# First-layer modulation columns: summed over the condition by TensorE, tile by tile, in place of VectorE, ScalarE and GpSimd

## The chip, the cores and the metric

The kernel runs on one core of one Trainium2 chip. The metric is device time in microseconds of one execution, lower is better. Engines are named as in the profile: PE is TensorE's products and PEld its weight loads, DVE is VectorE, ACT is ScalarE, POOL is GpSimd, SP is SyncE, which issues all the transfers.

## The reference

An encoder of two layers over 2048 tokens of 1024 channels. What matters here is the first step of a layer: a condition vector gives a shift and a scale for each channel and a gate.

```python
cond = jax.nn.silu(c)
for l in range(DEPTH):
    mod = cond @ ada_w[l] + ada_b[l]
    shift, scale, gate = jnp.split(mod, 3, axis=-1)
    h = x * (1.0 + scale[:, None]) + shift[:, None]
    ...
    x = layer_norm(DEEPNORM_ALPHA * x + (1.0 + gate[:, None]) * y, ln_g[l], ln_b[l])
```

`ada_w[l]` is 1024 x 3072. The first 2048 columns of `mod` are shift and scale; nothing of layer 0 can be multiplied before they are known. The projection of `h` that follows goes into two mixers (a gated linear recurrence and an RWKV-like one), and layer 1 is a gated recurrence behind a short convolution.

## The kernel before

Tokens go in two super-blocks of 1024, each in two halves (b = 0, 1) of 512; channels in eight tiles of 128 (k = 0 to 7). Each large product is done as three fast-float products of split operands (`mm3`, L431 to L433: high and low parts of both sides), so each input tile `h` is split into `hh` and `hl` by ScalarE and VectorE (`split`, L367 and L368) before TensorE may use it.

The start, which the change touches, is written in this order. A small matrix `wf` is folded from the low-rank weights: 32 f32 products of 256 columns into `pf` (L239), evacuated by ScalarE (L243). Then the columns of `ada_w[0]` come in four blocks of 512 columns (j), eight tiles `adw` of 128 x 512 f32 (256 KB) per block: blocks 0 and 2 first (shift and scale of channel tiles 0 to 3), then six x tiles, then blocks 1 and 3 (channel tiles 4 to 7), then the other x tiles. All are issued by SyncE in that order; 20 buffers hold `adw`, so the 21st tile waits until the first is used up.

`mod_start(j)` (L202) sums a block over the condition. Rows of a tile lie on partitions and one value of `cond` belongs to each, so a multiply by a per-partition scalar and an add over k leave a 128 x 512 sum per block: five of the eight k go through VectorE's multiply-add (`mod_add`, L166 and L168), three through ScalarE (L211, L213), two of which GpSimd adds up (L214), and VectorE joins both (L215). `mod_vec` (L186) then sums over the partitions on TensorE: four f32 products whose weights are 128 x 128 pieces of the sum and whose moving operand is one column of ones (L190). The result `pm`, 128 x 4, gets the bias in `mod_bias` (L175) and lies in `md`, from which ScalarE makes `h` (L401).

TensorE records two loads and two products for one such f32 product, so a call of `mod_vec` shows as eight records of each kind. The order on TensorE within a mixer is written by hand; at the start it is the scheduler's, from the order of the code and its priorities. The first projections are `pp_z` (96 products: two halves of the weights, two column tiles, two token halves); the first 18 need only blocks 0 and 2. The gate columns of layer 0 (blocks 4 and 5) and all of layer 1 keep the old way, later (`mod_cols`, L178, beside the mixer).

Of the kernel before, what the change touches and what calls it, by code (L numbers as in the profile page):

```python
# [13 lines left out]
F32 = mybir.dt.float32  # L14
# [3 lines left out]
AF = mybir.ActivationFunctionType  # L18
# [5 lines left out]
P = 128  # L24
D = 1024
KT = 8
BLK = 512
# [41 lines left out]
def tile_encoder(  # L69
# [19 lines left out]
    nc = tc.nc  # L89
# [27 lines left out]
    tp = _Cur()  # L117
    ps = ctx.enter_context(tc.tile_pool(name="ps", bufs=1, space=PSUM))
# [39 lines left out]
    cond = cst.tile([P, KT], F32, name="cond")  # L158
# [5 lines left out]
    def mod_add(acc, w, k, first):  # L164
        if first:
            nc.vector.tensor_scalar_mul(acc, w, cond[:, k : k + 1])  # L166
        else:
            nc.vector.scalar_tensor_tensor(  # L168
                out=acc, in0=w, scalar=cond[:, k : k + 1], in1=acc, op0=ALU.mult, op1=ALU.add
            )  # L170

    def mod_bias(l, j, pm):
        js = slice(4 * j, 4 * j + 4)
        o = VOFF[f"adb{l}"] + 4 * j
        nc.vector.scalar_tensor_tensor(  # L175
            out=md[l][:, js], in0=pm, scalar=0.0 if j < 2 else 1.0, in1=vec[:, o : o + 4], op0=ALU.add, op1=ALU.add
        )
# [8 lines left out]
    def mod_vec(l, j, acc):  # L186

        pm = ps.tile([P, 4], F32, name=f"pm{l}_{j}", tag="ta")
        for i in range(4):
            nc.tensor.matmul(pm[:, i : i + 1], acc[:, i * P : (i + 1) * P], ones, start=True, stop=True)  # L190
        mod_bias(l, j, pm)
# [9 lines left out]

    def mod_start(j):  # L202

        acc = [tp.tile([P, BLK], F32, name=f"acc0_{j}_{i}", tag=f"acc{i}", bufs=2) for i in range(2)]
        for k in range(KT):
            w = tp.tile([P, BLK], F32, name=f"adw0_{j}_{k}", tag="adw", bufs=20)
            nc.sync.dma_start(w, ada_w[0, k * P : (k + 1) * P, j * BLK : (j + 1) * BLK])
            if k not in (0, 2, 4):
                mod_add(acc[0], w, k, first=k == 1)
            elif k == 0:  # L210
                nc.scalar.activation(acc[1], w, AF.Identity, scale=cond[:, 0:1])  # L211
            else:
                nc.scalar.activation(w, w, AF.Identity, scale=cond[:, k : k + 1])  # L213
                nc.gpsimd.tensor_add(acc[1], acc[1], w)  # L214
        nc.vector.tensor_add(acc[0], acc[0], acc[1])  # L215
        return acc[0]

    x_first = []

    def x_tile(sb, b, k):  # L220
        src = up.tile([P, BLK + 3], F32, name=f"xt{sb}_{b}_{k}", tag="u")[:, 0:BLK]
        t0 = sb * SBT + b * BLK
        nc.sync.dma_start(src, xT[k, :, t0 : t0 + BLK])
        return src
# [11 lines left out]
    for k in range(KT):  # L236
# [5 lines left out]
            )  # L242
        nc.scalar.copy(wf[:, :, k], pf)  # L243

    accs = {j: mod_start(j) for j in (0, 2)}
    for j in (0, 2):
        mod_vec(0, j, accs[j])
    x_first += [x_tile(0, 0, k) for k in range(4)]
    x_first += [x_tile(0, 1, k) for k in range(2)]

    accs = {j: mod_start(j) for j in (1, 3)}
    for j in (1, 3):
        mod_vec(0, j, accs[j])

    def late_modulation_steps(l, js):

# [1109 lines left out]
```

## Time and profile before

| | us |
|---|---|
| median of three runs | 2450.46 |
| lowest and highest | 2445.37, 2455.84 |
| the profiled execution | 2446.24 |
| its span, first to last instruction | 2444.5 |
| TensorE busy in it | 2208.4 |
| mean granted TensorE clock (1 is 2.4 GHz) | 0.952 |

The profile is of one execution. Times in it are counted from the start of the span. A busy TensorE includes overlapped records, and a granted clock of 0.50 in a stretch means 1.2 GHz; a value between is a stretch in which it changed.

### The profile page before, as it was taken

To read this page: it belongs to the slowest core of one execution; us is meant where nothing else is said; L and a number is where in the kernel's file an instruction comes from. 1 tells how busy PE (TensorE), PEld (TensorE's weight loads), DVE (VectorE), ACT (ScalarE), POOL (GpSimd) and SP (SyncE) were. 2 spreads that over 40 slices of the span, in tenths; PEclk is the share of its full clock that TensorE was granted. 3 is DMA by queue.
4 is the path that set the end of the run, shared out by engine and by line. 5 is a ranking of instruction groups with operands and counts; after the bars stand their busy time and mean duration, and the time that the engine had idled before them with its cause. 6 is when DMAs were issued, how large, how long until landed. Compare 5 with 4: busy or idle time off the path is not lost. (4 is left out here: it accounts for less than half of the span.)

```text
span 2444.5 us, 45532 instructions
## 1 busy us (share of the span) xinstructions
PE 2208.4 (90%) x18400; PEld 1738.7 (71%) x18400; DVE 1454.8 (60%) x2697; ACT 1256.6 (51%) x2027; POOL 557.2 (23%) x586
## 2 busy tenths in 40 slices
PE   5989989999987998899999999989986999996998
PEld 4767767677766876677776777768765778774776
DVE  6546667566644677565666755356766156766166
ACT  4344556545566433454455556654666344666332
POOL 3311112111112222111111111122433232433231
PEclk7989999999998999999999999989998999998999
DMA  7310111111424645111111123254313544113542
GB/s 289 93 37 24 41 32 41 38 38 38 118 70 128 207 152 175 34 34 43 25 42 35 37 83 97 72 204 143 104 65 120 169 141 137 67 57 122 167 137 103
DMA packets 185938, 229.82 MB, mean 94 GB/s; under 512 B 65912, under 2 KB 99320, under 8 KB 185728
## 3 DMA queue, kind: packets, MB, share of 16 engines
q1 hardware_dynamic: 185728, 226.92, 29.1%
q8 instruction: 144, 2.36, 0.4%
q14 instruction: 66, 0.54, 0.1%
HBM read 175.46 MB, written 51.39 MB: 93 GB/s over the span
## 5 line engine op out<-in xcount | busy, mean ns | idle before, releaser
L431 PE MATMUL pp_g<-hl_h,wh_g 128*128 128x512 f32 x512 | 212.3, 415 | 40.8 <-ACT go L574 40.8
L433 PE MATMUL pp_g<-hh_h,wl_g 128*128 128x512 f32 x512 | 204.6, 400 | 2.0 <-POOL wl_g L368 2.0
L431 PE MATMUL po<-hl_wo,wh_mx 128*128 128x512 f32 x448 | 179.3, 400 | 28.9 <-DVE hl_wo L368 24.1
L432 PE MATMUL pp_g<-hh_h,wh_g 128*128 128x512 f32 x512 | 204.9, 400 | 0.0
L433 PE MATMUL po<-hh_wo,wl_mx 128*128 128x512 f32 x448 | 177.4, 396 | 0.0
L432 PE MATMUL po<-hh_wo,wh_mx 128*128 128x512 f32 x448 | 177.2, 396 | 0.0
L368 POOL TENSOR_TENSOR wl_g<-raw_g,wh_g 128x512 fp32r<-128x512 f32 x64 | 87.2, 1363 | 377.5 <-ACT wh_g L367 342.7
L431 PE MATMUL pp_b<-hl_h,wh_b 128*128 128x512 f32 x384 | 168.5, 439 | 5.0 <-ACT cr_b L805 5.0
L431 PE MATMUL pp_a<-hl_h,wh_a 128*128 128x512 f32 x384 | 168.7, 439 | 0.0
L432 PE MATMUL pp_b<-hh_h,wh_b 128*128 128x512 f32 x384 | 153.7, 400 | 0.0
L433 PE MATMUL pp_a<-hh_h,wl_a 128*128 128x512 f32 x384 | 153.5, 400 | 0.0
L432 PE MATMUL pp_a<-hh_h,wh_a 128*128 128x512 f32 x384 | 153.3, 399 | 0.0
L433 PE MATMUL pp_b<-hh_h,wl_b 128*128 128x512 f32 x384 | 153.0, 398 | 0.0
L431 PEld LDWEIGHTS pp_g<-hl_h,wh_g 128*128 128x128 f32 x512 | 99.5, 194 | 64.7 <-ACT go L574 41.7
L368 POOL TENSOR_TENSOR wl_a<-raw_a,wh_a 128x512 fp32r<-128x512 f32 x48 | 67.7, 1416 | 329.1 <-ACT wh_a L367 329.1
L568 DVE TENSOR_TENSOR go<-go,oi 128x512 f32<-128x512 f32 x64 | 46.8, 733 | 160.6 <-ACT go L564 144.9
L368 POOL TENSOR_TENSOR wl_mx<-raw_mx,wh_mx 128x512 fp32r<-128x512 f32 x64 | 80.7, 1265 | 269.1 <-ACT wh_mx L367 269.1
L368 POOL TENSOR_TENSOR wl_b<-raw_b,wh_b 128x512 fp32r<-128x512 f32 x48 | 66.5, 1391 | 271.1 <-ACT wh_b L367 270.1
L431 PEld LDWEIGHTS po<-hl_wo,wh_mx 128*128 128x128 f32 x448 | 86.0, 192 | 48.4 <-DVE hl_wo L368 24.9
L433 PEld LDWEIGHTS pp_g<-hh_h,wl_g 128*128 128x128 f32 x512 | 99.2, 194 | 25.2 <-POOL wl_g L368 3.5
L432 PEld LDWEIGHTS pp_g<-hh_h,wh_g 128*128 128x128 f32 x512 | 99.4, 194 | 19.2
L433 PE MATMUL pp_c<-hh_h,wl_c 128*128 128x512 f32 x256 | 102.2, 400 | 8.6 <-POOL wl_c L368 8.6
(355 smaller groups left out, 5707.4 us busy)
## 6 DMA issues: line engine op xcount, KB each, us to landing
adw<-in_ada_w_dram SPq DMA_DIRECT2D x96, 256.0 KB
oi<-o_dr SPq DMA_DIRECT2D x64, 256.0 KB
m_dr<-go SPq DMA_DIRECT2D x56, 256.0 KB
raw_b<-in_w_ev_dram SPq DMA_DIRECT2D x48, 256.0 KB
raw_a<-in_w_ev_dram SPq DMA_DIRECT2D x48, 256.0 KB
raw_g<-in_w_ev_dram SPq DMA_DIRECT2D x32, 256.0 KB
wo<-in_w_evo_dram SPq DMA_DIRECT2D x32, 256.0 KB
raw_mx<-m_dr SPq DMA_DIRECT2D x32, 256.0 KB
```

Of the source, the lines that this page charges most:

```text
L368: return (eng or nc.vector).tensor_tensor(out=lo, in0=src, in1=hi.bitcast(F32), op=ALU.subtract)
L431: nc.tensor.matmul(pt, ah, bl, start=first, stop=False)
L432: nc.tensor.matmul(pt, ah, bh, start=False, stop=False)
L433: nc.tensor.matmul(pt, al, bh, start=False, stop=last)
L568: nc.vector.tensor_mul(go[b], go[b], oi[b])
```

## The change

`mod_start` no longer makes a 128 x 512 sum. Each tile is used as weights as it lies: its four 128 x 128 pieces are loaded, the moving operand is column k of `cond`, and the eight k add up in the PSUM tile `pms`, 128 x 4. The bias goes on as before. Each block has a PSUM tag of its own, and `mod_vec` is no longer called for blocks 0 to 3 of layer 0.

```diff
     def mod_start(j):
 
-        acc = [tp.tile([P, BLK], F32, name=f"acc0_{j}_{i}", tag=f"acc{i}", bufs=2) for i in range(2)]
+        pm = ps.tile([P, 4], F32, name=f"pms_{j}", tag=("ta", "oa", "yb", "cg")[j])
         for k in range(KT):
             w = tp.tile([P, BLK], F32, name=f"adw0_{j}_{k}", tag="adw", bufs=20)
             nc.sync.dma_start(w, ada_w[0, k * P : (k + 1) * P, j * BLK : (j + 1) * BLK])
-            if k not in (0, 2, 4):
-                mod_add(acc[0], w, k, first=k == 1)
-            elif k == 0:
-                nc.scalar.activation(acc[1], w, AF.Identity, scale=cond[:, 0:1])
-            else:
-                nc.scalar.activation(w, w, AF.Identity, scale=cond[:, k : k + 1])
-                nc.gpsimd.tensor_add(acc[1], acc[1], w)
-        nc.vector.tensor_add(acc[0], acc[0], acc[1])
-        return acc[0]
+            for i in range(4):
+                nc.tensor.matmul(
+                    pm[:, i : i + 1], w[:, i * P : (i + 1) * P], cond[:, k : k + 1],
+                    start=k == 0 and i == 0, stop=k == KT - 1, skip_group_check=True,
+                )
+        mod_bias(0, j, pm)
...
-    accs = {j: mod_start(j) for j in (0, 2)}
     for j in (0, 2):
-        mod_vec(0, j, accs[j])
+        mod_start(j)
...
-    accs = {j: mod_start(j) for j in (1, 3)}
     for j in (1, 3):
-        mod_vec(0, j, accs[j])
+        mod_start(j)
```

The order that results, on TensorE, from the last fold to the first projection. Names carry layer or block and k (`adw0_0_1` is tile 1 of block 0), then a buffer number. Before:

```order
L239 MATMUL pf7_171<-lw_114,zw2_112 128x256
L239 MATMUL pf7_171<-lw_114,zw3_113 128x256
L190 MATMUL pm0_0_235<-ones_91,acc0_0_0_177 128x1 [waits DVE_49]
L190 MATMUL pm0_0_235<-ones_91,acc0_0_0_177 128x1 x3
L190 MATMUL pm0_2_241<-ones_91,acc0_2_0_206 128x1 [waits DVE_49,PE_49]
L190 MATMUL pm0_2_241<-ones_91,acc0_2_0_206 128x1 x3
L431 MATMUL pp_z0_1_0_547<-hl_h0_0_0_0_388,wh_z0_1_0_356 128x512 [waits DVE_49]
```

Changed, the last of the 16 tiles of blocks 0 and 2 and what follows:

```order
L209 MATMUL pms_2_227<-cond_106,adw0_2_6_264 128x1 [waits DMAHW4_49]
L209 MATMUL pms_2_227<-cond_106,adw0_2_6_264 128x1 x3
L209 MATMUL pms_2_227<-cond_106,adw0_2_7_270 128x1 [waits DMAHW5_49]
L209 MATMUL pms_2_227<-cond_106,adw0_2_7_270 128x1 x3
L426 MATMUL pp_z0_1_0_607<-hl_h0_0_0_0_448,wh_z0_1_0_416 128x512 [waits DVE_49]
L427 MATMUL pp_z0_1_0_607<-hh_h0_0_0_0_432,wh_z0_1_0_416 128x512 [waits Activation_49]
L428 MATMUL pp_z0_1_0_607<-hh_h0_0_0_0_432,wl_z0_1_0_417 128x512 [waits Pool_49]
L209 MATMUL pms_1_289<-cond_106,adw0_1_0_290 128x1 [waits DMAHW4_49]
L209 MATMUL pms_1_289<-cond_106,adw0_1_0_290 128x1 x3
L426 MATMUL pp_z0_1_0_607<-hl_h0_0_0_1_449,wh_z0_1_0_416 128x512
```

Where two bursts of four products stood, waiting for VectorE, there are now 64 products, each tile's first one waiting for its transfer; two of them stand earlier, between the second and the third fold. Six tiles of blocks 1 and 3 lie between the first 18 projections, the other ten stand behind them.

On VectorE, the last block before the split of the second token half (b = 1, k = 3). Before:

```order
L168 SCALAR_TENSOR_TENSOR acc0_3_0_288<-adw0_3_7_313,cond_106,acc0_3_0_288 128x512 [waits DMAHW3_49,DVE_49]
L215 TENSOR_TENSOR acc0_3_0_288<-acc0_3_0_288,acc0_3_1_289 128x512 [waits DVE_49,Pool_49]
L175 SCALAR_TENSOR_TENSOR md0_108<-pm0_3_323,vec_104 128x4 [waits PE_49]
L367 CAST hh_h0_0_1_3_383<-xt0_1_3_427 128x512 [waits Activation_49]
```

Changed:

```order
L363 TENSOR_TENSOR hl_h0_0_1_0_456<-xt0_1_0_285,hh_h0_0_1_0_440 128x512 [waits Activation_49]
L175 SCALAR_TENSOR_TENSOR md0_108<-pms_1_289,vec_104 128x4 [waits PE_49]
L175 SCALAR_TENSOR_TENSOR md0_108<-pms_3_339,vec_104 128x4 [waits PE_49]
L362 CAST hh_h0_0_1_3_443<-xt0_1_3_487 128x512 [waits Activation_49]
```

The adds are gone; the two writes of `md` follow one another directly, ahead of the split of tile 3 as the last one was before.

## Rows read from the trace of the kernel before

**Rows 1.** The page: span and instructions, then busy us of each engine.
```profile
span 2444.5 us, 45532 instructions
...
PE 2208.4 (90%) x18400; PEld 1738.7 (71%) x18400; DVE 1454.8 (60%) x2697; ACT 1256.6 (51%) x2027; POOL 557.2 (23%) x586
```

**Rows 2.** Timeline of PE: start us, length us, instructions, [idle before, who ended it].
```profile
9.34 15.06 PE L239 MATMUL pf<-lw,zw 128*128 128x256 f32 x60 [1.28 <-DMA zw<-in_w_zT_dram]
24.25 0.95 PE L190 MATMUL pm<-ones,acc 128*128 128x1 f32 x8
29.57 1.80 PE L190 MATMUL pm<-ones,acc 128*128 128x1 f32 x8 [4.37 <-DVE acc L215]
34.96 0.79 PE L431 MATMUL pp_z<-hl_h,wh_z 128*128 128x512 f32 x1 [3.60 <-DVE hl_h L368]
35.55 0.63 PE L432 MATMUL pp_z<-hh_h,wh_z 128*128 128x512 f32 x1
35.98 0.63 PE L433 MATMUL pp_z<-hh_h,wl_z 128*128 128x512 f32 x1
...
42.70 0.40 PE L433 MATMUL pp_z<-hh_h,wl_z 128*128 128x512 f32 x1
42.93 0.40 PE L431 MATMUL pp_z<-hl_h,wh_z 128*128 128x512 f32 x1
...
47.18 1.84 PE L190 MATMUL pm<-ones,acc 128*128 128x1 f32 x8 [3.06 <-DVE acc L215]
53.20 1.84 PE L190 MATMUL pm<-ones,acc 128*128 128x1 f32 x8 [4.18 <-DVE acc L215]
```

**Rows 3.** The same of PEld, TensorE's weight loads in three of the four bursts.
```profile
24.03 1.08 PEld L190 LDWEIGHTS pm<-ones,acc 128*128 128x128 f32 x8
29.54 1.74 PEld L190 LDWEIGHTS pm<-ones,acc 128*128 128x128 f32 x8 [4.43 <-issue]
...
47.15 1.78 PEld L190 LDWEIGHTS pm<-ones,acc 128*128 128x128 f32 x8 [3.75 <-issue]
```

**Rows 4.** The same of VectorE, to 94 us.
```profile
27.86 1.56 DVE L215 TENSOR_TENSOR acc<-acc,acc 128x512 f32<-128x512 f32 x1
31.40 0.16 DVE L175 SCALAR_TENSOR_TENSOR md<-pm,vec 128x4 f32<-128x4 f32 x1 [1.98 <-PE pm L190]
...
55.07 0.16 DVE L175 SCALAR_TENSOR_TENSOR md<-pm,vec 128x4 f32<-128x4 f32 x1 [2.02 <-PE pm L190]
...
92.38 0.75 DVE L797 SCALAR_TENSOR_TENSOR u_b<-pp_b,vec,u_b 128x511 f32<-128x511 f32 x1
93.04 1.53 DVE L168 SCALAR_TENSOR_TENSOR acc<-adw,cond,acc 128x512 f32<-128x512 f32 x2
```

**Rows 5.** Groups by line, 0 to 57 us: count, busy us, mean ns, idle before.
```profile
L168 DVE SCALAR_TENSOR_TENSOR acc<-adw,cond,acc 128x512 f32<-128x512 f32 x16 | 17.9, 1121 | 1.8 <-DMA adw<-in_ada_w_dram 1.5
...
L214 POOL TENSOR_TENSOR acc<-acc,adw 128x512 f32<-128x512 f32 x8 | 12.0, 1500 | 22.9 <-ACT adw L213 22.8
```

**Rows 6.** SyncE's queue: start us, us, transfers issued.
```profile
21.89 10.39 SPq L207 DMA_DIRECT2D adw<-in_ada_w_dram  x16
```

**Rows 7.** Stretches: length, busy us (records) by engine, granted clock, DMA share, GB/s.
```profile
29.50:30.00 0.50, 0.43 (x3) 0.46 (x3) 0.00 (x0) 0.00 (x0) 0.50 (x1) 0.62 1.07 393
...
39.00:40.00 1.00, 1.00 (x4) 0.63 (x2) 1.00 (x1) 1.00 (x3) 0.92 (x2) 0.57 1.06 389
40.00:41.00 1.00, 0.24 (x2) 0.00 (x0) 1.00 (x2) 1.00 (x2) 1.00 (x1) 1.00 1.02 389
...
43.00:44.00 1.00, 1.00 (x4) 0.35 (x2) 0.96 (x2) 0.10 (x1) 0.92 (x2) 0.64 1.05 428
...
48.00:49.00 1.00, 1.00 (x5) 0.93 (x5) 0.00 (x0) 0.00 (x0) 0.00 (x0) 0.50 0.00 0
...
206.00:209.00 3.00, 2.34 (x38) 1.75 (x37) 2.99 (x8) 2.19 (x4) 0.00 (x0) 1.00 0.04 8
...
210.00:213.00 3.00, 2.86 (x17) 2.44 (x18) 1.64 (x5) 0.00 (x0) 0.00 (x0) 0.59 0.00 0
```

## The prediction

> **What bounds the kernel now.** I read the page first: TensorE is busy 90% of a span of 2444.5 us, no other engine over 60% [rows 1]. A share says nothing about the first 60 us, where the change lies, so I went on to the timeline of that stretch, engine by engine. There TensorE is the engine that waits. It folds the low-rank weights until 24.40 (9.34 + 15.06), then does four short bursts of eight records (29.57, 47.18, 53.20 and one at 24.25), and each but the first begins with idle time that VectorE's `acc` ends: 4.37, 3.06 and 4.18 us [rows 2]. VectorE is the last of the three adding engines: 16 multiply-adds at 1121 ns, though the same step takes 0.75 us when GpSimd is quiet, and GpSimd's own eight adds take 1500 ns each [rows 4, 5]. SyncE issues the second 16 tiles from 21.89 to 32.28 [rows 6], and 256 KB at the 389 GB/s of these stretches is 0.67 us a tile [rows 7], so the tiles are there long before the sums.
>
> Two moments count. The first is the end of the second burst, 31.37 (29.57 + 1.80): the shift and scale of blocks 0 and 2 are written at 31.40 [rows 4], and the first projection starts at 34.96, 3.59 us later [rows 2]. The second is the end of the fourth burst, 55.04 (53.20 + 1.84): the last columns are written at 55.07. From there the order of all five engines differs in some 40 rows of the next 45 us, and after that in none. So the question is one number: when does the last modulation product end, against 55.04? What it moves, moves everything behind it, because the rest is one chain through TensorE with waits that start from the same products.
>
> **The change part by part.** *Removed:* 16 + 4 + 4 steps on VectorE, 12 on ScalarE, 8 on GpSimd and 16 products on TensorE (32 records). On VectorE alone that is 16 x 1.12 us = 18 us [rows 5]. All of it lies before 55.04, and the only thing it bought was that moment; nothing behind it gets shorter for it. The accumulators' memory is freed too, which costs and gains nothing where SyncE is already ahead.
>
> *Added:* 32 tiles x 4 products of one column, each two load-and-product records as in the old bursts: 256 records, where 32 were. The old bursts are the same instruction (128x128 f32 weights, one moving column), so their rows price it. At the granted clock of 0.5 eight loads take 1.74 and 1.78 us [rows 3]: 1.78 / 8 = 0.2225 us is an upper bound; without the last load's own length (the eight span seven steps, and one second of such a burst holds parts of five records [rows 7]) 0.21 remains. I take 0.213. At clock 1.00 eight take 1.08 us, 0.135 each as an upper bound; half of the slow value, 0.107, is a lower one, and I take 0.115. So a tile of eight records costs TensorE 1.70 us at 1.2 GHz and 0.92 at 2.4, against 0.67 for its arrival. TensorE becomes the engine that the tiles wait for, whatever the clock.
>
> The Trainium skill prices a weight load in "TensorE: Matmul & The Clock Gate", section "LDWEIGHTS (loading the stationary operand)", as its columns divided by 1.2 GHz, 107 ns for 128 columns. The burst at 1.00 comes near it, the bursts at 0.5 take twice as much, so the measurement decides; by the page's 107 ns at every clock the rival without a fall, below, would be the forecast, with some 2 us less.
>
> *The clock* decides between the two prices. It fell to 0.5 at about 29.6, 4.4 us after the last record at 25.20, and at about 43.3, some 3 us after the first projections stopped at 40.24, although wide products ran again by 42.70; it rose, at 39.9, only after some 5 us of unbroken 512-column products from 34.96 [rows 2, 7]. During the bursts at 47 and 53 it stayed at 0.50. No row shows a long run of one-column products, so I bound it by the nearest: at 206 to 209 TensorE was busy 2.34 of 3.00 us, 1.75 of it with weight loads, much of it for narrow products, and the clock fell right after, in the stretch from 210 [rows 7]. Being busy with loads did not hold it there. I take it that the run of one-column products counts as a pause: the clock falls about 4 us after the last wide product and stays at 0.5 until wide products run unbroken.
>
> *The sum.* Two of the first tile's products go between the second and third fold, while TensorE waits for a copy: 0. The other 124 records of blocks 0 and 2 start at 24.25. Until 28.4 (24.40 + 4) at 0.115: 36 records. The other 88 at 0.213: 18.7 us, to 47.1. Then the unchanged 3.59 us until the first split input: 50.7. TensorE then has 18 projection products and 128 records of blocks 1 and 3, interleaved, and both inputs and tiles are there. At 0.5 a product starts every 0.43 us (35.55 to 35.98 [rows 2]): 7.7 us; 128 x 0.213 = 27.3 us; sum 85.7. Against 55.04: **+30.7 us**. The upper price, 0.2225, would make it +33, the lower one +29.
>
> *Moved:* on VectorE the writes of blocks 1 and 3 now stand ahead of the split of inputs (b1, k2 and k3), so these wait for TensorE's last tile. They did so before: they stood behind the adds, and only ran after 55.07. So 0. Further on, the first lerp of the projection `b` (92.38) now stands behind the late gate's two last adds, which followed it before (93.04, 1.53 us) [rows 4]; ScalarE's copy and TensorE's next group wait for it: 0 to 1.5 us, I take 0.5. The extra wait of SyncE on TensorE (tile 20 on needs a freed buffer; x tiles, then weights, queue behind it) ends with tile 11's products, by about 41 at 0.213, some 40 us before the last tile is used; hidden, and if that cover went it would be DMA at 0.67 us a tile.
>
> Sum: 2446.2 (the profiled execution, 2444.5 of it span) + 31.2 = 2477.4. That execution is 4.2 us under the median of the three runs, 2450.5, from which the same step gives 2481.7. I take the middle, 2479.
>
> **The rivals.** *A, the clock holds (not slower).* If records without a pause keep TensorE at 2.4 GHz, the sum is 24.25 + 124 x 0.115 = 38.5, + 3.59 = 42.1, + 18 x 0.23 (42.70 to 42.93 [rows 2]) + 128 x 0.115 = 61.0: +5.9, with up to 2 us more if the pause of 3.59 lets the clock fall for a while, and 0.5 from the lerp: 2453 to 2459. For it speaks that the loads run back to back; against it the fall after 206 to 209. It decides at a mean price of 0.138 us a record: below, the 252 records behind 24.25 (252 p - 22.6 us with the fast products) stay within 0.5%, 12 us, about what a measurement of this kernel can tell from no change; at 0.09 the change would be even. The Trainium skill, "TensorE: Matmul & The Clock Gate", "Why this matters for your kernels", speaks for A: it asks only that no idle gaps stand between bursts of matmuls. Its "Part 4: PE-mode transpose" speaks against it, since transposes are said not to count as busy in the same way.
>
> *B, the clock wakes half way.* The first 62 products run as in the forecast (to 50.7), then the interleaved projections bring the clock up after some 5 us: 5 us at half price, the rest at full, about 21 instead of 35 us; +17, 2465. The 18 wide products never stand more than four in a row there, which speaks against it.
>
> *C, the products are nearly free (faster).* If a tile were taken as it lands, the last one would end near 40 and everything would move by -15 us. That needs records of 0.03 us; every burst says three times that at least.
>
> *D, nothing takes place as told.* Were the projections not held by the last tile (another order), the loss would be the first half's 16 us alone. The order of the queues excludes it: the projections of b1 k2 stand behind all 32 tiles.
>
> **How the numbers follow.** The forecast 0.68; A 0.17; B 0.10; C 0.02; dearer than the forecast's upper price, because of waits between tiles that no row shows, 0.03. The range: the forecast spans +29 to +33 on 2446 to 2456 (the runs before reach 2455.8), so 2475 to 2489; downwards it takes in B and half of A: 2456 to 2490. Left out are C, half of A and most of the dear case, about 0.15. Faster by over 0.5%: 0.02. Within: A, 0.17, and a bit of B's low end, 0.18. Slower: 0.80.
>
> **What would show it.** In the profile after: the first 24 us as before; then one unbroken run of one-column products on TensorE with the granted clock falling to 0.5 about 4 us into it, steps of 1.7 us a tile, the first projection at about 51 instead of 34.96, the last modulation write near 86 instead of 55.07, VectorE, ScalarE and GpSimd nearly idle between 24 and 47, and from there the same rows shifted by a constant 31. A clock of 1.00 in 30 to 40 makes A right and the forecast wrong; a clock of 1.00 in 60 to 85 alone makes it B. A later stage that wins the loss back would show as a shift that shrinks along the span, and I see no idle time there that is not itself chained to the start.

## The result, and the profile after

The changed kernel took 2474.01 us (median of four runs, 2471.88 to 2486.45), the one before, beside it, 2447.91 us (four runs, 2444.61 to 2455.84). The ratio, here and below worked out from the single runs and not from the medians, is 1.0112, with a 95% interval of 1.007 to 1.0155: slower, by 17 to 38 us. The forecast was 2479, with a range of 2456 to 2490.

The profiled execution took 2471.88 us. First the page's lines that answer to [rows 1]: 224 more records of each kind on TensorE (256 for 32), 39 us more of TensorE and 27 us less of VectorE.

```profile
span 2470.1 us, 45907 instructions
...
PE 2247.3 (91%) x18624; PEld 1779.1 (72%) x18624; DVE 1427.6 (58%) x2673; ACT 1249.6 (51%) x2015; POOL 542.8 (22%) x578
```

The timeline of PE at the start answers to [rows 2]: start, length, instructions, and in brackets the idle time before and who ended it.

```profile
12.41 10.61 PE L236 MATMUL pf<-lw,zw 128*128 128x256 f32 x48
22.85 22.03 PE L209 MATMUL pms<-cond,adw 128*128 128x1 f32 x124
48.48 0.80 PE L426 MATMUL pp_z<-hl_h,wh_z 128*128 128x512 f32 x1 [3.59 <-DVE hl_h L363]
...
49.92 1.70 PE L209 MATMUL pms<-cond,adw 128*128 128x1 f32 x8
...
66.56 17.06 PE L209 MATMUL pms<-cond,adw 128*128 128x1 f32 x80
85.60 0.80 PE L426 MATMUL pp_z<-hl_h,wh_z 128*128 128x512 f32 x1 [1.98 <-DVE hl_h L363]
```

The reader should see two solid blocks where [rows 2] had four bursts of eight: 124 records without a pause in the first, and 18 projections with tiles between them, then 80 records in a row, in the second. 17.06 / 80 is 0.2133 us a record. The same of VectorE shows the two writes that answer to 31.40 and 55.07 in [rows 4]:

```profile
44.92 0.16 DVE L175 SCALAR_TENSOR_TENSOR md<-pms,vec 128x4 f32<-128x4 f32 x1 [13.49 <-PE pms L209]
...
83.66 0.16 DVE L175 SCALAR_TENSOR_TENSOR md<-pms,vec 128x4 f32<-128x4 f32 x1 [13.49 <-PE pms L209]
```

VectorE now waits for TensorE, not TensorE for VectorE. The last write is 28.6 us later than before. Five stretches (length, busy us and records of PE, PEld, DVE, ACT, POOL, then the granted clock, DMA share and GB/s) tell the price:

```profile
23.00:27.00 4.00, 4.00 (x39) 4.00 (x38) 0.00 (x0) 2.03 (x4) 2.85 (x3) 1.00 1.06 392
...
27.50:28.00 0.50, 0.50 (x5) 0.50 (x5) 0.00 (x0) 0.00 (x0) 0.36 (x1) 0.71 1.04 381
27.50:44.00 16.50, 16.50 (x80) 16.50 (x80) 0.16 (x1) 0.00 (x0) 0.36 (x1) 0.51 0.75 256
50.00:66.00 16.00, 16.00 (x63) 14.75 (x62) 2.07 (x4) 2.93 (x5) 0.00 (x0) 0.50 0.48 169
67.00:83.00 16.00, 16.00 (x76) 16.00 (x77) 0.16 (x1) 0.00 (x0) 0.00 (x0) 0.50 0.00 0
```

The clock falls from 1.00 (2.4 GHz) to 0.50 (1.2 GHz) at 27.7, 4.7 us after the last fold. Of the first block's 124 records some 80 fit in behind that at 0.213 us, so the other 44 took the 4.9 us ahead of it: 0.11 us each. (4.00 / 39 would be less, but a row also counts the records that only reach into its stretch.) The clock stays at 0.50 until wide projections have run alone again, from 85.60 to 89.1, although TensorE is busy every microsecond of the stretches shown.

### The profile page after: what moved, and what is told of

Read it like the earlier page. It is cut to its first block, busy times and chain, and to the rows that moved or that the text cites. A ratio compares the mean times of both kernels' runs of the same rounds, so it can differ in the third digit from the quotient of the medians.

```text
span 2470.1 us, 45907 instructions
## 1 busy us (share of the span) xinstructions
PE 2247.3 (91%) x18624; PEld 1779.1 (72%) x18624; DVE 1427.6 (58%) x2673; ACT 1249.6 (51%) x2015; POOL 542.8 (22%) x578
## 5 line engine op out<-in xcount | busy, mean ns | idle before, releaser
L426 PE MATMUL po<-hl_wo,wh_mx 128*128 128x512 f32 x448 | 179.5, 401 | 29.6 <-DVE hl_wo L363 25.3
L426 PEld LDWEIGHTS po<-hl_wo,wh_mx 128*128 128x128 f32 x448 | 86.1, 192 | 49.4 <-DVE hl_wo L363 26.1
```

Of the source, the lines that this page charges most:

```text
L426: nc.tensor.matmul(pt, ah, bl, start=first, stop=False)
```

## Where the rest of the time went

The start lost 28.6 us, the span only 25.6. ScalarE's timeline has the same two instructions in both kernels, first of before, then of the changed one:

```profile
163.46 0.58 ACT L1155 COPY u_a<-pp_a 128x512 f32<-128x512 f32 x1 [5.08 <-PE pp_a L433]
...
216.34 0.69 ACT L795 ACTIVATE u_b<-pp_b,omu 128x512 f32<-128x512 f32 x1 [7.58 <-PE pp_b L433]
```

```profile
192.37 0.58 ACT L1150 COPY u_a<-pp_a 128x512 f32<-128x512 f32 x1 [5.08 <-PE pp_a L428]
...
241.67 0.69 ACT L790 ACTIVATE u_b<-pp_b,omu 128x512 f32<-128x512 f32 x1 [6.01 <-PE pp_b L428]
```

The copy is 28.9 us late, the next `u_b` 25.3 us. PE's timeline shows where a part of that went, again first of before:

```profile
174.32 0.80 PE L431 MATMUL pp_a<-hl_h,wh_a 128*128 128x512 f32 x1
...
178.75 0.63 PE L432 MATMUL pp_a<-hh_h,wh_a 128*128 128x512 f32 x1
179.18 0.63 PE L433 MATMUL pp_a<-hh_h,wl_a 128*128 128x512 f32 x1
...
180.36 0.50 PE L431 MATMUL pp_b<-hl_h,wh_b 128*128 128x512 f32 x1
```

```profile
202.60 0.80 PE L426 MATMUL pp_a<-hl_h,wh_a 128*128 128x512 f32 x1
...
206.20 0.40 PE L427 MATMUL pp_a<-hh_h,wh_a 128*128 128x512 f32 x1
206.44 0.39 PE L428 MATMUL pp_a<-hh_h,wl_a 128*128 128x512 f32 x1
...
207.37 0.50 PE L426 MATMUL pp_b<-hl_h,wh_b 128*128 128x512 f32 x1
```

The same twelve products and one small group take 6.04 us in before (a product starts every 0.43 us to the end) and 4.77 us here (every 0.23 us from 205.28 on): the clock rose earlier. The stretch at 210 of [rows 7], where before fell to 0.59, is another such place; here it runs at full clock:

```profile
237.60:240.60 3.00, 3.00 (x23) 2.18 (x20) 1.57 (x3) 0.00 (x0) 0.00 (x0) 1.00 0.08 11
```

Nothing in the change touches that work; it met the low clock in one execution and not in the other. Further on the shift of equal instructions goes up and down by such steps, between 25 and 31 us, and ends at 25.6.

## The experiments

Each kernel was timed beside the one before on the same chip. "Last write" is the start of the last `md` write in its profile (before 55.07).

**e1_half.** Is the price a product's or a tile's?

```diff
-            for i in range(4):
+            for i in (0, 1) if k % 2 == 0 else (2, 3):
...
```

> Two of a tile's four one-column products are left out (columns 0 and 1 of even tiles, 2 and 3 of odd ones; the modulation comes from half the tiles, all 32 still arrive and are waited for). Theory (records at the clock's price): 62 records from 22.85, of which 40 at 0.105 us until the clock falls at 27.1 and 22 at 0.213: blocks 0 and 2 written near 31.9, first projection 35.5, then 18 x 0.43 + 64 x 0.213 = 21.4: the last modulation write near 57 (after: 83.7, before: 55.1), and a time 27 us below the changed kernel's, within 5 us of the one before. Rival (the price is a tile's: its arrival, its wait, its buffer): the last write stays near 84 and the time 25 us above the one before.

Measured: 2447.67 us against 2451.41, ratio 0.9982 (0.997 to 0.9995). PE's first block, then VectorE's last write:

```profile
24.24 10.75 PE L209 MATMUL pms<-cond,adw 128*128 128x1 f32 x60
```

```profile
60.12 0.16 DVE L175 SCALAR_TENSOR_TENSOR md<-pms,vec 128x4 f32<-128x4 f32 x1 [6.67 <-PE pms L209]
```

The last write moved from 83.66 to 60.12 with all tiles still arriving and waited for: the price belongs to the product. It is 3 us later than expected: 1.4 of them because the folds ended later here, at 24.4, and about 1 because the clock fell earlier, at 26.5 (0.97 from 26.0 to 26.5, then 0.50). The time, though, came out below before's, 9 us less than the last write says; e9_three takes that up.

**e2_first and e3_second.** One pair of blocks on TensorE, the other by the three engines as before.

```diff
     for j in (0, 2):
         mod_start(j)
...
-    for j in (1, 3):
-        mod_start(j)
+    accs = {j: mod_start_old(j) for j in (1, 3)}
+    for j in (1, 3):
+        mod_vec(0, j, accs[j])
```

(e3_second has it the other way round.)

> Only blocks 0 and 2 go to TensorE, blocks 1 and 3 are summed by the three engines as before. Theory (each part pays for its own products): blocks 0 and 2 written at 44.9 as in the changed kernel (+13.5), then the old 23.7 us to the last write, since VectorE's adds for blocks 1 and 3 stand behind that write: 68.6, +13.5 us, 2461. Rival (the second part was limited by VectorE, so the adds, whose tiles are long there, take less than before): 60 to 64, +5 to +9.

> Only blocks 1 and 3 go to TensorE, blocks 0 and 2 are summed by the three engines as before. Theory: blocks 0 and 2 written at 31.3 as before, first projection at 35, then 18 x 0.43 + 128 x 0.213 = 35.0 at the low clock: last write near 70, +15 us, 2463; with the run before the two halves add up to the changed kernel's +28.6. Rival (the clock, which before had come up at 39.9 in this stretch, comes up here too, because one half of the products is not preceded by the long run): 15 us less, +2 to +6.

Measured: 2466.01 us, ratio 1.0062 (1.0042 to 1.0083), and 2466.71 us, ratio 1.0072 (1.0052 to 1.0093). VectorE's last write of e2_first, then of e3_second:

```profile
68.18 0.16 DVE L175 SCALAR_TENSOR_TENSOR md<-pm,vec 128x4 f32<-128x4 f32 x1 [2.02 <-PE pm L190]
```

```profile
69.04 0.16 DVE L175 SCALAR_TENSOR_TENSOR md<-pms,vec 128x4 f32<-128x4 f32 x1 [13.49 <-PE pms L225]
```

+13.1 and +14.0 us at the last write, together 27.1 of the changed kernel's 28.6: the two halves pay for themselves, as the theory said, and neither rival holds.

**e7_fill128.** Does a wide operand between them keep the clock up?

```diff
...
+                nc.tensor.matmul(fill[0:1, 0:128], cond[:, k : k + 1], w[:, i * P : i * P + 128], start=True, stop=True)
```

> The changed kernel with one more product behind each one-column product: the same 128x128 piece of the tile as the moving operand (128 columns) against one column of weights, into a bank that nobody reads. It doubles the records on TensorE (512 where 256 were), the new ones with a wide moving operand. Theory (the granted clock sets the price of a one-column product, and what holds the clock is wide moving operands): the clock stays at 1.00, a tile takes 8 x 0.107 + 8 x 0.107 = 1.7 us, as much as in the changed kernel, and the time stays within 5 us of the changed kernel's (the last write 80 to 88), although twice the work is done; the one-column records take 0.11 us instead of 0.21. Rival (a one-column product costs 0.21 us whatever the clock, or the clock stays at 0.5): a tile takes 2.6 to 3.4 us, the last write comes at 110 to 138, and the time is +55 to +82 us.

Measured in two runs: 2540.28 us, ratio 1.0373 (1.035 to 1.0395), last write 151.18. The stretches, then PE's timeline, each second row of it, at either clock:

```profile
24.00:27.00 3.00, 3.00 (x22) 1.80 (x20) 0.00 (x0) 2.03 (x4) 1.74 (x2) 1.00 1.01 368
40.00:60.00 20.00, 20.00 (x79) 11.51 (x78) 0.16 (x1) 0.00 (x0) 0.00 (x0) 0.50 0.23 66
120.00:140.00 20.00, 20.00 (x79) 11.29 (x79) 0.00 (x0) 0.00 (x0) 0.00 (x0) 0.50 0.00 1
```

```profile
24.17 0.38 PE L215 MATMUL fill<-adw,cond 128*1 128x128 f32 x2
...
24.79 0.38 PE L215 MATMUL fill<-adw,cond 128*1 128x128 f32 x2
...
30.17 0.59 PE L215 MATMUL fill<-adw,cond 128*1 128x128 f32 x2
...
31.20 0.59 PE L215 MATMUL fill<-adw,cond 128*1 128x128 f32 x2
```

The theory's condition failed: the clock fell in spite of the added products, as in the rival, but the loss (+89 us, last write 151) lies beyond the rival's range too (+55 to +82, 110 to 138). Busy all the time, half of the records with 128 moving columns, and still 0.50 for over 110 us. Both sides had the price too low: a pair of products, four records, takes 0.62 us even at 1.00 (24.17 to 24.79) and 1.03 us at 0.50 (30.17 to 31.20), so a tile takes 2.5 or 4.1 us, where the theory had 1.7 and the rival 2.6 to 3.4. What a one-column record alone takes at full clock can't be told from these pairs; the next run shows it.

**e8_full.** The same with added products that look like the folds.

```diff
...
+                nc.tensor.matmul(
+                    fill[:, 0:256], w[:, i * P : (i + 1) * P], lw[:, i].rearrange("p a c -> p (a c)"), start=True, stop=True
+                )
```

> The changed kernel with one more product behind each one-column product, as in the run before (e7_fill128), but with the whole 128x128 piece as weights and 256 moving columns (like the weight folds, during which the clock was 1.00), into a bank that nobody reads; all 32 tiles now stand ahead of the first projection. Theory (the clock sets the price of a one-column product; e7_fill128 failed because its added products used one column of weights): the clock stays at 1.00 from 23 to 105, a tile takes 8 x 0.107 + 8 x 0.215 = 2.6 us, the last modulation write comes near 105 and the time is +50 to +57 us. Rival (one-column products pull the clock down whatever stands between them): at 0.5 a tile takes 5.2 us, the last write comes near 180 and the time is +125 to +140 us. Second rival (the clock stays at 1.00 but a one-column record still takes 0.21 us): 3.4 us a tile, last write near 131, +80 us.

Measured in one run: 2498.73 us, +51 on the median of 2447.9; last write 108.14. The stretches, then PE's timeline of one pair of products:

```profile
26.00:60.00 34.00, 34.00 (x209) 31.31 (x208) 0.16 (x1) 1.56 (x3) 3.72 (x3) 1.00 0.60 191
60.00:105.00 45.00, 45.00 (x277) 41.44 (x276) 7.21 (x14) 9.43 (x15) 0.00 (x0) 1.00 0.10 31
```

```profile
40.36 0.28 PE L211 MATMUL pms<-cond,adw 128*128 128x1 f32 x2
40.50 0.68 PE L215 MATMUL fill<-lw,adw 128*128 128x256 f32 x2
41.02 0.28 PE L211 MATMUL pms<-cond,adw 128*128 128x1 f32 x2
```

The clock stays at 1.00 throughout. One pair starts 0.66 us after the other; two records of 256 columns are 0.44 of that (48 of them took 10.52 us in this profile's folds), so the one-column record takes 0.11 us. The clock sets its price, and both rivals are out (+125 and +80). With twice the records the last write is 24 us behind the changed kernel's, 43 ahead of e7_fill128's. Between e7_fill128 and e8_full two things differ, 1 or 128 columns of weights and 128 or 256 moving columns; which of them counts was not separated, so the reason that the expectation gives for e7_fill128 is not shown.

**e4_wide.** The same sums with the tile as the moving operand.

```diff
...
+            nc.tensor.matmul(pr[0:1], cond[:, k : k + 1], w, start=k == 0, stop=k == KT - 1)
+        row = tp.tile([P, BLK], F32, name=f"row_{j}", tag="row", bufs=2)[0:1]
+        nc.vector.tensor_copy(row, pr[0:1])
+        pm = ps.tile([P, 4], F32, name=f"pms_{j}", tag="tb", bufs=2)
+        for i in range(4):
+            nc.tensor.matmul(pm[:, i : i + 1], row[:, i * P : (i + 1) * P], ones[0:1], start=True, stop=True)
```

> The same sums on TensorE in another form: the column of the condition is the weights (128x1) and the tile moves, 512 columns at once; 32 products of two records in place of 128. The row of 512 sums is copied by VectorE and turned into four columns by four products with one row of weights. All 32 tiles stand ahead of the first projection. At clock 1.00 a record of 512 columns starts every 0.43 us (twice a 256-column fold record's 0.22): 0.86 us a tile, 16 tiles from 23 to 37, 32 to 50.5, last modulation write near 52.5, the 18 projection products behind it at 0.23 until 55: before has 56.96 at that point, so -2 to -4 us, 2446. If the clock falls here as in e7_fill128 (one column of weights): 1.72 us a tile after 27, all tiles by 74, the projections by 82, +23 to +26 us, 2475, as the changed kernel.

Measured: 2448.47 us against 2447.9, ratio 1.0 (0.9992 to 1.0009). PE's first block, VectorE's last write, and three stretches:

```profile
23.91 7.03 PE L208 MATMUL pr<-adw,cond 128*1 128x512 f32 x16
```

```profile
56.03 0.16 DVE L175 SCALAR_TENSOR_TENSOR md<-pms,vec 128x4 f32<-128x4 f32 x1 [1.43 <-PE pms L213]
```

```profile
24.00:40.00 16.00, 16.00 (x49) 4.44 (x48) 1.63 (x4) 2.03 (x4) 3.72 (x3) 1.00 0.93 324
40.00:54.00 14.00, 14.00 (x39) 3.41 (x38) 7.58 (x16) 9.49 (x15) 0.00 (x0) 1.00 0.70 242
56.00:90.00 34.00, 32.90 (x142) 26.20 (x142) 27.55 (x73) 12.10 (x20) 13.97 (x27) 1.00 0.49 154
```

0.44 us a record at full clock; the clock, which before was at 0.50 at 48 [rows 7], never falls until after 90. So one column of weights alone does not bring it down. The last write is 3.5 us later than I expected: the folds ended at 23.9 and not 23, and the products that turn a row into columns (eight records, 1.05 us) took TensorE's time between the blocks. TensorE does all the adding here, at no loss of time: the form of the products, not the engine, made the change expensive.

**e5_vec and e10_joint.** The other way: VectorE alone, without ScalarE and GpSimd. The edit of e5_vec; e10_joint also puts the sums of two blocks side by side in PSUM and adds their biases in one write.

```diff
-            if k not in (0, 2, 4):
-                mod_add(acc[0], w, k, first=k == 1)
...
+            mod_add(acc, w, k, first=k == 0)
```

> The other way: before, with all 32 tiles summed by VectorE alone; ScalarE's scalings and GpSimd's adds are left away. Theory (of before's price on VectorE, 1121 ns a step, the part over 0.75 is GpSimd's adds beside it): 16 steps of a pair take 12 us, the first pair from 13.2 to 25.5 and its burst to 27.5 (before 31.4); then VectorE has 12 us of steps and 5 us of input splits from 29 on, and the last write comes near 48.5 (before 55.1): -6 us, 2445. Rival (VectorE is the bound, twelve more steps cost what they cost): at 1.1 us a step the pair takes 17.6 us, the last write comes near 62: +7 us.

> e5_vec (VectorE alone sums all 32 tiles) with one bias write for a pair of blocks in place of one for each, so that VectorE's steps for the second block don't wait for TensorE's burst for the first (1.61 us idle in the first pair, 0.55 in the second). Theory: blocks 0 and 2 written at 27.3 (28.75 in e5_vec), the last write at 47.5 (49.4), -7.5 us against before, -2 against e5_vec, 2441 to 2443. Rival (TensorE's bursts for the two blocks now run one after the other at the end of each pair): the second burst was last there anyhow, so the write can't be later than in e5_vec; the gain is then nought, -5 us against before.

Measured: e5_vec 2443.05 us against 2447.9, ratio 0.9977 (0.9964 to 0.9989); e10_joint 2440.36 us against 2452.72, ratio 0.9953 (0.9934 to 0.9973). Both beat both kernels, the one before by only 0.2 and 0.5%. VectorE's group by line, 0 to 57 us, of e5_vec and then of e10_joint (count, busy us, mean ns), and e10_joint's last write:

```profile
L168 DVE SCALAR_TENSOR_TENSOR acc<-adw,cond,acc 128x512 f32<-128x512 f32 x28 | 22.8, 817 | 0.9 <-DMA adw<-in_ada_w_dram 0.2
```

```profile
L168 DVE SCALAR_TENSOR_TENSOR acc<-adw,cond,acc 128x512 f32<-128x512 f32 x28 | 20.9, 751 | 1.0 <-DMA adw<-in_ada_w_dram 0.3
```

```profile
46.20 0.17 DVE L221 TENSOR_TENSOR md<-pm,vec 128x8 f32<-128x8 f32 x1 [1.96 <-PE pm L219]
```

28 steps take 21 to 23 us where 16 took 17.9 [rows 5]. Without GpSimd's adds a step costs 817 and 751 ns, not 1121, and the last write comes at 49.41 and 46.20, near the theories' 48.5 and 47.5; the first rival's 62 is out, and so is the second's, that one write for two gains nothing. The Trainium skill says in "SBUF — State Buffer", "Who interferes with whom", that VectorE and GpSimd share one pair of ports as "an exclusive lock"; the trace agrees: before's three steps from 15.93 took 1.52 us each, twice their 0.75, while GpSimd had three operations of its own between 15.31 and 19.93 (two adds and the split of a weight tile).

```profile
15.93 4.56 DVE L168 SCALAR_TENSOR_TENSOR acc<-adw,cond,acc 128x512 f32<-128x512 f32 x3 [0.58 <-DMA adw<-in_ada_w_dram]
```

**e6_vt02.** Two of eight tiles on TensorE, six on VectorE.

```diff
...
+            if k in (0, 2):
+                for i in range(4):
+                    nc.tensor.matmul(
+                        pm[:, i : i + 1], w[:, i * P : (i + 1) * P], cond[:, k : k + 1],
+                        start=k == 0 and i == 0, stop=False, skip_group_check=True,
+                    )
+            else:
+                mod_add(acc, w, k, first=first)
...
```

> A small share for TensorE: of each block's eight tiles two (k = 0 and 2) are summed by TensorE as in the changed kernel, six by VectorE alone, whose accumulator joins the same bank with four products against ones; ScalarE's scalings and GpSimd's adds are left away. Theory: VectorE's 12 steps of a pair end near 22.7, when the last tile is there; TensorE has 32 + 16 records from 23, at 0.107 us 5.1 us: blocks 0 and 2 written at 28.5 (before 31.4); then 9 us of steps and 5 us of splits on VectorE and 32 + 16 records and 18 projections on TensorE: last write near 47 (before 55.1): -8 us, 2443. Rival (one-column products beside the projections pull the clock down and give back what VectorE wins): last write 53 to 57, -2 to +2 us.

Measured: 2443.68 us against 2447.9, ratio 0.9972 (0.996 to 0.9984). VectorE's last two writes, then a stretch:

```profile
46.55 0.16 DVE L175 SCALAR_TENSOR_TENSOR md<-pms,vec 128x4 f32<-128x4 f32 x1 [5.56 <-PE pms L220]
...
53.00 0.16 DVE L175 SCALAR_TENSOR_TENSOR md<-pms,vec 128x4 f32<-128x4 f32 x1 [1.96 <-PE pms L220]
```

```profile
28.00:44.00 16.00, 12.41 (x41) 10.77 (x42) 9.26 (x16) 7.92 (x12) 0.94 (x1) 0.50 1.05 393
```

The last write is 6 us later than expected and at the edge of the rival's 53 to 57: the clock stood at 0.50 from 28 to 44, block 1's bias write waited 5.56 us for TensorE, and block 3's six steps stood behind it in VectorE's queue. So the rival had the clock right, though not the time. Waits of this kind (1.61 and 0.55 us in e5_vec) are what e10_joint's single write removes. The time was 4 us better than before all the same, as much as e5_vec's, from a last write 3.6 us later than there.

**e9_three.** A point between e1_half and the changed kernel.

```diff
             for i in range(4):
+                if i == k % 4:
+                    continue
...
```

> The changed kernel with three of a tile's four products (one in turn is left out, so a quarter of the sum is missing): a point between e1_half, whose last write was 5 us later than before's and whose time was 4 us shorter, and the changed kernel. Theory (time follows the last modulation write, within the spread of the clock's falls): 94 records from 22.85, 40 of them until 27.1, the others at 0.213 until 38.6; first projection 42.2; 18 x 0.43 + 96 x 0.213 = 28.2: last write 70.4, +15 us, the time +11 to +20 us. Rival (a late start is partly given back in what follows, about 8 us of it, as e1_half seems to say): last write at 70 too, but the time only +5 to +9 us.

Measured: 2459.66 us (2453.2 to 2471.09) against 2452.72, ratio 1.0041 (1.0019 to 1.0062). The last write, where it was expected (70.4):

```profile
70.18 0.16 DVE L175 SCALAR_TENSOR_TENSOR md<-pms,vec 128x4 f32<-128x4 f32 x1 [10.08 <-PE pms L211]
```

The price is right to 0.2 us, the time is not settled: +5 to +15 us by the interval holds both theories. All runs together, last write against before (55.07) and difference of the medians:

| kernel | last write, us | median, us |
|---|---|---|
| e10_joint | -8.9 | -12.4 |
| e5_vec | -5.7 | -4.9 |
| e6_vt02 | -2.1 | -4.2 |
| e4_wide | +1.0 | +0.6 |
| e1_half | +5.1 | -3.7 |
| e2_first | +13.1 | +14.6 |
| e3_second | +14.0 | +15.3 |
| e9_three | +15.1 | +6.9 |
| the change | +28.6 | +26.1 |
| e8_full (one run) | +53.1 | +50.8 |
| e7_fill128 | +96.1 | +88.9 |

The time follows the last write, within -9 and +2 us. The two that fall 8 to 9 us short, e1_half and e9_three, don't make a case for the rival, since e2_first and e3_second, nearly as late as e9_three, give nothing back. Much of it comes from putting a write of one execution beside a median: before's profiled execution, 2446.24 us, lies 5.2 and 6.5 us under the medians that the two were timed against. In their own executions (spans of 2445.3 and 2456.3 us against 2444.5) e1_half ends 0.8 and e9_three 11.8 us after before, 4.3 and 3.3 less than their last writes say, while e2_first (2468.6) ends 24.1 after it, 11.0 more than its own says. Their profiles show only the known kind of steps. Both leave out part of the sums, so what follows works on other values; whether that matters was not tested. Runs of one kernel spread over 10 us and more.

## Why the prediction was right, step by step

- *The moment that counts.* Right: shown by e2, e3 and the table, to within the 9 us told there.
- *Price at the low clock*, taken as 0.213: measured 0.2133. *At the high clock*, taken as 0.115 with a lower bound of 0.107: 0.11 in the changed kernel and in e8_full. Only the 44 or so records ahead of the fall paid it.
- *The clock falls some 4 us after the last wide product and stays down.* Right: last fold at 23.02, the fall at 27.7; in e1_half it came 2.1 us after the last fold. But the ground for it was thin, and here the forecast had some luck. The row that was to show a TensorE busy with loads losing the clock, 206 to 209, has wide products in its first microsecond, and between it and the fall lies a row with TensorE idle for two thirds:

```profile
209.00:210.00 1.00, 0.32 (x2) 0.13 (x2) 1.00 (x2) 0.00 (x0) 0.00 (x0) 1.00 0.02 8
```

So that fall spoke as well for rival A, in which only a pause costs the clock. The case without a pause was first shown by the changed kernel. With 1.00 nowhere in 30 to 40 or in 60 to 85, rivals A and B are both wrong. A's price at full clock was right (0.11 in e8_full); its condition was not met. C fails by the price, over three times its 0.03 even at full clock, and D by the row at 85.60: the projections did wait for the last tile. The Trainium skill asks, in "TensorE: Matmul & The Clock Gate", "Why this matters for your kernels", only that no idle gaps stand between bursts; the trace differs, with 16.00 of 16.00 us busy at 0.50.
- *End of the first half*, 47.1: 44.88. Of the 2.2 us, 1.4 are the folds, which ended at 23.0 and not 24.40; most of the rest is the clock, which fell 4.9 us into the run and not 4.15. "The first 24 us as before" was wrong, though not by the change: the folds ended at 22.0 in e3_second and at 24.4 in e1_half.
- *First projection 3.59 us later*: 48.48 - 44.88 = 3.60. *Second half*, 35.0 us: 83.62 - 48.48 = 35.1.
- *The lerp behind the two late adds*, 0.5 us: TensorE's wait ahead of `pp_b` grew from 5.04 to 5.53. PE's row of before, then of the changed kernel:

```profile
93.37 0.80 PE L431 MATMUL pp_b<-hl_h,wh_b 128*128 128x512 f32 x1 [5.04 <-ACT cr_b L805]
```

```profile
122.57 0.79 PE L426 MATMUL pp_b<-hl_h,wh_b 128*128 128x512 f32 x1 [5.53 <-ACT cr_b L800]
```

- *A constant +31 from there.* Wrong: +28.6 at the last write, +29.2 at 93, +25.3 at 216, +25.6 at the end. I had ruled out a shrinking shift because no idle time was left to win back; I had not thought of the clock's falls, which don't come at the same work in every execution. It is a matter of a few us, up or down.
- *The price of the old way.* The forecast took before's 55.04 as given. e5_vec and e10_joint show that the help of ScalarE and GpSimd was itself a small loss; what the prediction noted in passing (0.75 against 1.12 us a step) was the better change.

## What to carry to other kernels

Here a product with one moving column cost TensorE two weight loads, 0.22 us at the high clock and 0.43 at the low one, and in an unbroken run of them the clock fell to 0.50 and stayed there. Look for such rows in the profile before pricing a run of them at the high clock, and try the large operand as the moving one: in e4_wide the clock stayed at 1.00. Before giving TensorE work that other engines do, find which instant their work really holds up, and ask first whether two of those engines are slowing each other.

## What the runs showed of the hardware that I had not expected

- A clock of 0.50 over 110 us of unbroken records (e7_fill128), half of them with 128 moving columns, which no pause explains; and 1.00 with 512 moving columns against one column of weights (e4_wide).
- Of two kernels with 512 records each, the one with the wider added products ends its sums 43 us sooner (108 in e8_full, 151 in e7_fill128).
